# Transposing on VectorE in blocks of 32 instead of on TensorE, in a hybrid decoder step

## The chip, the cores and the metric

The kernel runs on one core of a Trainium2 chip. The metric is the device time of one execution in microseconds (us); lower is better. The core has five engines with a queue each: PE (TensorE, matmuls; its weight loads are shown as PEld), DVE (VectorE), ACT (ScalarE), POOL (GpSimd) and SP (SyncE, which here issues nearly all transfers). An engine works its queue in order and waits on semaphores where an operand or a buffer is not ready.

## The reference, cut to what matters

One step of a decoder layer with two head groups: 512 prompt tokens in one sequence, and 8 x 8 sample tokens with a past of 1024 positions each in a paged cache.

```
h = rms_norm(x, norm_in);  z = h @ w_in          # all branches from one projection (2048 -> IN_WIDTH)
attention heads (8 x 128): indexer scores -> top-k mask -> softmax -> @ v     # prompt, and samples with their cache
GLA heads (4 of 128 x 256): S = exp(last)*S + (k*exp(last-cum))^T v ;  o = (q*exp(cum)) S + (masked q k decay) v
y = rms_norm(x + concat(att * silu(ga), rms_norm(o, gla_norm) * silu(gb)) @ w_out, norm_f)
```

It returns y for prompt and samples, the new keys and values and the new states. The change touches the samples' softmax weights on their way to the product with v, the GLA heads' outputs on their way to the gate, and the store of the samples' y.

## The kernel before, in words

**Projection.** Activations stand transposed (features on partitions; 576 columns: 512 prompt, 64 sample). `gemm(b)` makes one block of 128 output features with matmuls of 128x288, each product in three terms (high and low halves of both operands, line L222); a weight tile of 128x512 serves 24 of them. The v columns are made the other way round with matmuls of 512 columns (L616 to L618). `wload` brings each weight tile: SP loads `w_raw` (L178), ACT rounds it to `w_hi` (L181), DVE makes the rest `w_lo` (L184); there are 3 raw buffers and 5 of each half.

**Sample units.** `units(un, hg, pages)` runs for `hg` 0 and 1 and in each for `w` 0 and 1: four units, each with 128 rows (4 heads x 32 sample rows) by 1088 columns (1024 of the past, 64 own). The scores `pS` are copied to `pr`, one ACTIVATE takes the exponentials with their sum (L813), nine PE transposes of 128x128 turn them (L821 eight times, L824 once) into PSUM tiles `pt`, three ACT copies (L822, L825) bring them to `prT`, and the `pOs` matmuls (L255, L258) multiply them with v.

**GLA heads.** `recur(h)` runs for h = 0 to 3. Its first half is the chain over the prompt's four chunks (`pUg` L1113, `pO`, state `Sst`). Then for each of the eight sample sequences b:

```
Kb = gl.tile([96, P], F32R, name="Kb", bufs=2)
ve.tensor_scalar(out=Kb, in0=ks[b // 4]..., scalar1=bm[...], op0=ALU.mult)        # L1145, DVE
pe.matmul(pU[:, :DV], Kb, vs[b // 4], start=True, stop=True)                       # L1146, PE: pUg
ve.scalar_tensor_tensor(out=st[:, m, :], in0=st[:, m, :], ..., in1=pU[:, :DV])     # L1147, DVE: st
```

With two buffers the `Kb` of a sequence can be made when the `pUg` two before it is done. The head ends with five scalings of `osb` (L1156, DVE), ten PE transposes (L1161 eight times, L1164 twice), four ACT activations into `oT` (L1162, L1165; tag e0, two buffers) and two stores `so` into scratch memory (SP). `gate(i)` later loads them again as `mo` into buffers of the same tag e0 (SP, L948) and multiplies them into `og` (POOL, L949). The decays `lv_d` that the next head's `pl` matmuls read are made on POOL (L969, L970), ACT (L971) and DVE (L1028, L1029).

**End.** The output projection writes the rows `y` in five row tiles, the sample rows last; each is normalised and stored in pieces of 512 columns (L1312 on DVE, L1314 on ACT, stores L1315).

**Order.** A tile scheduler fixes each engine's order when the kernel is built, from a timeline of its own and from priorities (`wload` goes ahead); nothing is reordered on the chip. PE, DVE, ACT, POOL and SP each follow their list.

Of the kernel before, what the change touches and what calls it, by code (L numbers as in the profile page):

```python
# [10 lines left out]
F32 = mybir.dt.float32  # L11
# [4 lines left out]
AF = mybir.ActivationFunctionType  # L16
ALU = mybir.AluOpType
AX = mybir.AxisListType
PSUM = bass.MemoryType.PSUM

P = 128
D = 2048
NK = D // P
TP = 512
# [95 lines left out]
def build(tc, I, O):  # L120
# [130 lines left out]
    def mm1(name):  # L251
        return pm.tile([P, 512], F32, name=name, tag="pm")
# [493 lines left out]

    mixS = gaS

    def units(un, hg, pages):


# [23 lines left out]
        for w in range(2):  # L775
            qz = ev.tile([P, 4, 4, 32], F32, name="qz", tag="e0", bufs=2)
            po_.memset(qz, 0.0)
            for g in range(4):
                src = qaS[:, 4 * hg + g, 32 * w : 32 * w + 32].rearrange("p (b t) -> p b t", t=DT)
                dst = qz[:, g].rearrange("p b t -> p (b t)")  # L780
                dst = bass.AP(tensor=dst.tensor, offset=dst.offset, ap=[dst.ap[0], [40, 4], [1, DT]])
                po_.tensor_copy(dst, src)
            pr = un.tile([P, PAST + TS], F32, name="pr")
            mx = un.tile([P, 8], F32, name="mxs", bufs=2)
            lsel = [selw[:, 256 * half + P * w : 256 * half + P * (w + 1)] for half in range(2)]
            for half in range(2):
                S = pm.tile([P, 512], F32, name="pS", tag="pu", bufs=1)
                pe.matmul(S, lsel[half], biasS[:, :512], start=True, stop=False)
                mms = []
                for bb in range(4):  # L790
                    k4 = kv[bb].rearrange("p j (g s) -> p j g s", g=4)
                    mms[:0] = [
                        partial(pe.matmul, S[32 * g : 32 * g + 32], qz[:, g, bb, :], k4[:, :, g, :], start=False, stop=(bb == 0), tile_position=(0, 32 * g))
                        for g in range(4)
                    ]
                run(*mms)
                yield
                kv = fetch(w, half, 1 - half)
                se.copy(pr[:, 512 * half : 512 * half + 512], S)
                ve.reduce_max(out=mx[:, half : half + 1], in_=pr[:, 512 * half : 512 * half + 512], axis=AX.X)  # L800
                if not half:
                    yield from rest(3)
            S = pm.tile([P, 512], F32, name="pS", tag="pu", bufs=1)
            pe.matmul(S[:, :TS], lsel[1], biasS[:, 512:], start=True, stop=False)
            run(*(
                partial(pe.matmul, S[32 * g : 32 * g + 32, :TS], qaS[:, 4 * hg + g, 32 * w : 32 * w + 32], kaS[:, 4 * hg + g, :], start=False, stop=True, tile_position=(0, 32 * g))
                for g in range(4)
            ))
            se.copy(pr[:, PAST:], S[:, :TS])
            ve.reduce_max(out=mx[:, 2:3], in_=pr[:, PAST:], axis=AX.X)  # L810
            ve.reduce_max(out=mx[:, 3:4], in_=mx[:, 0:3], axis=AX.X)
            ve.tensor_scalar(out=mx[:, 3:4], in0=mx[:, 3:4], scalar1=-SCALE, scalar2=None, op0=ALU.mult)
            se.activation(pr, pr, AF.Exp, bias=mx[:, 3:4], scale=SCALE, accum_out=mx[:, 4:5])  # L813
            ve.reciprocal(out=mx[:, 7:8], in_=mx[:, 4:5])
            yield
            prT = un.tile([P, 9, P], F32, name="prT")
            for c in range(3):
                pt = mm1("pt")
                if c < 2:
                    for j in range(4):  # L820
                        pe.transpose(pt[:, P * j : P * (j + 1)], pr[:, 512 * c + P * j : 512 * c + P * (j + 1)], ident)  # L821
                    se.copy(prT[:, 4 * c : 4 * c + 4, :], pt.rearrange("p (j r) -> p j r", j=4))  # L822
                else:
                    pe.transpose(pt[:, :P], pr[:, PAST + TS - P :], ident)  # L824
                    se.copy(prT[:, 8, :], pt[:, :P])  # L825
            yield from rest(2)
            pO = pm.tile([P, 512], F32, name="pOs", tag="pu", bufs=1)
            for half in range(2):
                mms = []
                for j in range(4):  # L830
                    mms[:0] = [
                        partial(
                            pe.matmul, pO[32 * g : 32 * g + 32].rearrange("p (b d) -> p b d", b=4), prT[:, 4 * half + j, 32 * g : 32 * g + 32],
                            kv[j][:, :, P * g : P * (g + 1)], start=(not half and j == 3), stop=False, tile_position=(0, 32 * g),
                        )
                        for g in range(4)
                    ]
                if half:
                    mms += [
                        partial(  # L840
                            pe.matmul, pO[32 * g : 32 * g + 32].rearrange("p (b d) -> p b d", b=4), prT[:, 8, 32 * g : 32 * g + 32],
                            vaS[:, P * h : P * (h + 1)].unsqueeze(1).to_broadcast([P, 4, P]), start=False, stop=True, tile_position=(0, 32 * g),
                        )
                        for g in range(4) for h in (4 * hg + g,)
                    ]
                run(*mms)
                yield
                if not half:
                    kv = fetch(w, 1, 1)
                    yield from rest(3)  # L850
                elif w == 0:
                    kv = fetch(1, 0, 0)
            ob = pr[:, :512]
            se.activation(ob, pO, AF.Copy, scale=mx[:, 7:8])
            pt = mm1("pt")
            for bb in range(4):
                pe.transpose(pt[:, P * bb : P * (bb + 1)], ob[:, P * bb : P * (bb + 1)], ident)
            src = bass.AP(tensor=pt.tensor, offset=pt.offset, ap=[pt.ap[0], [32, 4], [P + DT, 4], [1, DT]])
            sl = (slice(None), slice(4 * hg, 4 * hg + 4), slice(32 * w, 32 * w + 32))
            ve.tensor_tensor(  # L860
                out=mixS[sl].rearrange("p g (b t) -> p g b t", t=DT), in0=src,
                in1=gaS[sl].rearrange("p g (b t) -> p g b t", t=DT), op=ALU.mult,
            )
            yield from rest(2 + (w < hg))
# [227 lines left out]
    def recur(h, eL, qE, kDt, ks):  # L1092
# [61 lines left out]
        ve.reciprocal(out=ss, in_=ss)  # L1154
        for i in range(5):
            ve.tensor_scalar(out=osb[:, i, :], in0=osb[:, i, :], scalar1=ss[:, i : i + 1], scalar2=None, op0=ALU.mult)  # L1156
        for half in range(2):
            o_t = ev.tile([P, T], F32, name="oT", tag="e0", bufs=2)
            pt = mm1("pt")
            for i in range(4):  # L1160
                pe.transpose(pt[:, P * i : P * (i + 1)], osb[:, i, P * half : P * (half + 1)], ident)  # L1161
            se.activation(o_t[:, :TP], pt, AF.Copy, scale=gnorm[:, half : half + 1])  # L1162
            pt = mm1("pt")
            pe.transpose(pt[:, :P], osb[:, 4, P * half : P * (half + 1)], ident)  # L1164
            se.activation(  # L1165
                o_t[:, TP:T].rearrange("p (m c) -> p m c", m=4), pt[:, :P].rearrange("p (m c) -> p m c", m=4)[:, :, 0:16],
                AF.Copy, scale=gnorm[:, half : half + 1],
            )
            sy.dma_start(spill_o[2 * h + half], o_t)
# [73 lines left out]
    mg_s.close()  # L1243
    fp, fp_s = pool("fin", 1, side="right")
    y = [[None] * 5 for _ in range(4)]
    for n in range(20):
        if n < 16:
            y[n // 5][n % 5] = xp.tile([P, T], F32, name="y", tag=("xh", "xl")[n % 2])
        else:
            y[n // 5][n % 5] = fp.tile([P, 512], F32, name=f"y{n}")  # L1250
# [31 lines left out]
    for q, (c0, n) in enumerate(CH):  # L1282
# [14 lines left out]
        for i in range(5):  # L1297
# [5 lines left out]
            if last:  # L1303
# [2 lines left out]
                se.activation(yr[:r, i : i + 1], yr[:r, i : i + 1], AF.Sqrt, bias=eps[:r], scale=1.0 / D)  # L1306
                ve.reciprocal(out=yr[:r, i : i + 1], in_=yr[:r, i : i + 1])
                dst = O["yp"][P * i : P * (i + 1), :] if i < 4 else O["ys"]
                for c in range(4):
                    yc = y[c][i][:r, :512]  # L1310
                    if c < 2:
                        ve.tensor_scalar(out=yc, in0=yc, scalar1=yr[:r, i : i + 1], scalar2=None, op0=ALU.mult)  # L1312
                    else:
                        se.activation(yc, yc, AF.Copy, scale=yr[:r, i : i + 1])  # L1314
                    (sy, sy, se, sy)[c].dma_start(dst[:, 512 * c : 512 * c + 512], yc)  # L1315
# [79 lines left out]
```

## Time and profile before

| | |
|---|---|
| median of 3 runs | 1227.73 us (1227.54 to 1228.92) |
| profiled execution | 1227.91 us, span of its trace 1226.1 us, mean TensorE clock 0.998 |
| PE busy | 1212.5 us (99%) |
| DVE, ACT, POOL busy | 662.0 us (54%), 561.9 us (46%), 300.3 us (24%) |

The span runs from the first to the last instruction of the core. Busy time counts an engine's instructions, not its waits. Times in the trace are counted from the span's start. In a timeline a row is the start, the length, engine, line, operation and operands; `x8` puts consecutive equal instructions together, and the brackets behind it give the idle time before and what ended it.

### The profile page before, as it was taken

The page shows a single profiled execution, that of the slowest core. Times are in us where ns is not written, and L with a number is a line of the kernel's source. Part 1 is how long each engine was busy: PE and PEld are TensorE (multiplying, and loading weights), DVE is VectorE, ACT ScalarE, POOL GpSimd, SP SyncE. Part 2 cuts the span into 40 slices and gives each one's busy share as a digit, 9 for nine tenths or more (in the row PEclk, how much of TensorE's full clock was granted, in tenths as well). Part 3 has the DMA queues.
Part 4 walks back from the last instruction along what each step waited for, and adds up shares of the span by engine and source line. Part 5 has one row for each costly group of instructions (what it writes and reads, how often), then busy time and mean ns, then how long its engine had stood idle before and what let it go on. Part 6 is the DMA issues. An engine that isn't in the chain of part 4 may idle for free.

```text
span 1226.1 us, 23589 instructions
## 1 busy us (share of the span) xinstructions
PE 1212.5 (99%) x8693; PEld 1072.7 (87%) x8699; DVE 662.0 (54%) x1327; ACT 561.9 (46%) x1076; POOL 300.3 (24%) x471
## 2 busy tenths in 40 slices
PE   9999999999999999999999999999999999999997
PEld 8999987899997879998887788688899998888897
DVE  6777899699843314444436344436465552223233
ACT  6986655453443323443335363454466542223234
POOL 2225666446411201010104220302124010202021
PEclk9999999999999999999999999999999999999999
DMA  9643233423457586665557583677435544333335
GB/s 307 241 130 102 72 107 102 161 86 105 148 188 240 188 297 214 217 215 182 187 195 231 195 314 128 229 259 229 134 100 164 171 152 136 107 97 122 89 115 176
DMA packets 126885, 209.42 MB, mean 171 GB/s; under 512 B 14497, under 2 KB 37554, under 8 KB 126066
## 3 DMA queue, kind: packets, MB, share of 16 engines
q1 hardware_dynamic: 125826, 206.60, 50.9%
q8 instruction: 68, 1.11, 0.4%
q10 hardware_dynamic: 944, 1.32, 0.3%
q14 instruction: 47, 0.39, 0.1%
HBM read 184.52 MB, written 23.22 MB: 169 GB/s over the span
## 4 chain that ended last, share of the span: by engine, by line
PE 90%; DVE 5%; DMA 3%; ACT 1%; issue 1%; POOL 0%; SPq 0%; DVEq 0%; ACTq 0%; POOLq 0%
PE ps_g L222 37%; PE ps_g L230 6%; PE acc L1261 5%; PE acc L1259 5%; PE acc L1260 5%; PE ps_g L616 5%; PE ps_g L617 5%; PE ps_g L618 5%; PE pOs L258 2%; PE pS L258 2%; PE acc L1264 1%; PE acc L1263 1%; DMA xr<-in_xT 1%; PE ps_v L612 1%; PE ps_v L613 1%; DVE wk L505 1%
## 5 line engine op out<-in xcount | busy, mean ns | idle before, releaser
L181 ACT CAST w_hi<-w_raw 128x512 fp32r<-128x512 f32 x316 | 194.0, 619 | 360.5 <-PE ps_g L222 126.3
L184 DVE TENSOR_TENSOR w_lo<-w_raw,w_hi 128x512 fp32r<-128x512 f32 x252 | 180.1, 718 | 320.5 <-ACT w_hi L181 317.9
L222 PE MATMUL ps_g<-xl,w_hi 128*128 128x288 f32 x1312 | 289.0, 299 | 0.0
L222 PE MATMUL ps_g<-xh,w_hi 128*128 128x288 f32 x1312 | 288.2, 299 | 0.3 <-ACT xh L211 0.3
L222 PE MATMUL ps_g<-xh,w_lo 128*128 128x288 f32 x1312 | 286.0, 297 | 0.0
L222 PEld LDWEIGHTS ps_g<-xh,w_hi 128*128 128x128 f32 x1312 | 213.0, 189 | 6.0 <-issue 2.5
L222 PEld LDWEIGHTS ps_g<-xl,w_hi 128*128 128x128 f32 x1312 | 213.4, 189 | 1.7 <-issue 0.4
L222 PEld LDWEIGHTS ps_g<-xh,w_lo 128*128 128x128 f32 x1312 | 212.5, 188 | 0.6
L1260 PE MATMUL acc<-w_lo,mh 128*128 128x512 f32 (+1 forms) x320 | 110.7, 346 | 0.0
L1261 PE MATMUL acc<-w_hi,ml 128*128 128x512 f32 (+1 forms) x320 | 110.7, 346 | 0.0
L1259 PE MATMUL acc<-w_hi,mh 128*128 128x512 f32 (+1 forms) x320 | 110.3, 346 | 0.0
L616 PE MATMUL ps_g<-w_hi,xh 128*128 128x512 f32 x256 | 101.4, 397 | 0.0
L184 POOL TENSOR_TENSOR w_lo<-w_raw,w_hi 128x512 fp32r<-128x512 f32 x64 | 86.3, 1351 | 60.9 <-ACT w_hi L181 47.6
L617 PE MATMUL ps_g<-w_lo,xh 128*128 128x512 f32 x256 | 100.2, 391 | 0.0
L618 PE MATMUL ps_g<-w_hi,xl 128*128 128x512 f32 x256 | 99.8, 390 | 0.0
L1279 POOL TENSOR_TENSOR y<-y,nfb 128x512 f32<-128x512 f32 (+3 forms) x25 | 27.5, 1113 | 190.1 <-ACT yjk L1278 190.1
L1260 PEld LDWEIGHTS acc<-w_lo,mh 128*128 128x128 f32 x320 | 60.5, 189 | 7.5
L1259 PEld LDWEIGHTS acc<-w_hi,mh 128*128 128x128 f32 x320 | 60.4, 189 | 7.5
L1261 PEld LDWEIGHTS acc<-w_hi,ml 128*128 128x128 f32 x320 | 60.4, 189 | 7.5
L616 PEld LDWEIGHTS ps_g<-w_hi,xh 128*128 128x128 f32 x256 | 48.1, 188 | 12.7 <-issue 1.7
L618 PEld LDWEIGHTS ps_g<-w_hi,xl 128*128 128x128 f32 x256 | 48.1, 188 | 10.1
L617 PEld LDWEIGHTS ps_g<-w_lo,xh 128*128 128x128 f32 x256 | 48.1, 188 | 9.4
(340 smaller groups left out, 1941.7 us busy)
## 6 DMA issues: line engine op xcount, KB each, us to landing
w_raw<-in_w SPq DMA_DIRECT2D x188, 256.0 KB, 2.9
kt<-in_ck SPq DMA_DIRECT2D x128, 256.0 KB, 5.3
vt<-in_cv SPq DMA_DIRECT2D x128, 256.0 KB, 5.3
w_raw<-in_wv SPq DMA_DIRECT2D x64, 256.0 KB, 3.0
w_raw<-in_wo SPq DMA_DIRECT2D x64, 256.0 KB, 2.7
xr<-in_xT SPq DMA_DIRECT2D x16, 288.0 KB, 4.8
xt<-in_xp SPq DMA_DIRECT2D x4, 1024.0 KB, 5.5
sv<-v_tok SPq DMA_DIRECT2D x16, 256.0 KB, 4.9
```

What stands on the lines that cost most here:

```text
L181: c = se.copy(hi, raw)
L184: lo_eng[0].tensor_tensor(out=lo, in0=raw, in1=hi.bitcast(F32), op=ALU.subtract)
L222: pe.matmul(ps[:, j, :HT], wt, xt[:, j * HT : (j + 1) * HT], start=(k == 0 and n == 0), stop=(k == NK - 1 and n == 2),)
L230: pe.matmul(ps[:, 0, :TQ], wt[:, c], xt[:, P:T], start=(k == 0 and n == 0), stop=(k == NK - 1 and n == 2))
L258: f()
L616: pe.matmul(accs[i], xh[k][:, c], wh, start=a, stop=False)
L617: pe.matmul(accs[i], xh[k][:, c], wl, start=False, stop=False)
L618: pe.matmul(accs[i], xl[k][:, c], wh, start=False, stop=b)
L1259: pe.matmul(acc, mh[k][:, tsl], wh, start=(k == 0), stop=False)
L1260: pe.matmul(acc, mh[k][:, tsl], wl, start=False, stop=False)
L1261: pe.matmul(acc, ml[k][:, tsl], wh, start=False, stop=(k == NK - 1))
L1279: po_.tensor_tensor(out=yc, in0=yc, in1=nfb[:r, cs], op=ALU.mult)
```

## The change

- `blocks32` is new: 16 DVE transposes, each of a strip of 32 partitions whose blocks of 32 columns it turns.
- Units: `pr` gets 64 zero columns (POOL) between the past and the own columns, so that it is nine tiles of 128; the exponentials are two ACTIVATEs whose sums one DVE addition joins; `blocks32` of 32x9x32 writes `prT` in place of nine PE transposes and three ACT copies.
- Heads: `blocks32` of 32x8x32 writes the four prompt chunks of `osb` into the buffer of `vtok`, another of 32x2x32 writes the sample rows into that of `kDt`; the `oT` activations read those, so the next head's load into `vtok` and copy into `kDt` wait for them. Ten PE transposes per head go.
- End: the samples' `y` is one tile; 1152 columns are scaled on DVE and stored by SP, 896 on ACT and stored by ACT's queue.

```diff
+    def blocks32(out, src):
+        for a in range(4):
+            for c in range(4):
+                ve.transpose(out[32 * c : 32 * c + 32, :, 32 * a : 32 * a + 32], src[32 * a : 32 * a + 32, :, 32 * c : 32 * c + 32])
...
-            pr = un.tile([P, PAST + TS], F32, name="pr")
+            pr = un.tile([P, PAST + P], F32, name="pr")
+            po_.memset(pr[:, PAST : PAST + TS], 0.0)
...
-            se.activation(pr, pr, AF.Exp, bias=mx[:, 3:4], scale=SCALE, accum_out=mx[:, 4:5])
+            se.activation(pr[:, :PAST], pr[:, :PAST], AF.Exp, bias=mx[:, 3:4], scale=SCALE, accum_out=mx[:, 4:5])
+            se.activation(own_p, own_p, AF.Exp, bias=mx[:, 3:4], scale=SCALE, accum_out=mx[:, 5:6])
+            ve.tensor_tensor(out=mx[:, 4:5], in0=mx[:, 4:5], in1=mx[:, 5:6], op=ALU.add)
...
-            for c in range(3):
-                pt = mm1("pt")
-                if c < 2:
-                    for j in range(4):
-                        pe.transpose(pt[:, P * j : P * (j + 1)], pr[:, 512 * c + P * j : 512 * c + P * (j + 1)], ident)
-                    se.copy(prT[:, 4 * c : 4 * c + 4, :], pt.rearrange("p (j r) -> p j r", j=4))
-                else:
-                    pe.transpose(pt[:, :P], pr[:, PAST + TS - P :], ident)
-                    se.copy(prT[:, 8, :], pt[:, :P])
+            blocks32(prT, pr.rearrange("p (j s) -> p j s", s=P))
...
+        flat = lambda x: x.rearrange("p i d -> p (i d)").rearrange("p (j t) -> p j t", t=P)
+        blocks32(flat(vtok), flat(osb[:, :4]))
+        blocks32(kDt[:, :2], flat(osb[:, 4:]))
+        turn = flat(vtok).rearrange("p (i two) t -> p two i t", two=2)
         for half in range(2):
             o_t = ev.tile([P, T], F32, name="oT", tag="e0", bufs=2)
-            pt = mm1("pt")
-            for i in range(4):
-                pe.transpose(pt[:, P * i : P * (i + 1)], osb[:, i, P * half : P * (half + 1)], ident)
-            se.activation(o_t[:, :TP], pt, AF.Copy, scale=gnorm[:, half : half + 1])
-            pt = mm1("pt")
-            pe.transpose(pt[:, :P], osb[:, 4, P * half : P * (half + 1)], ident)
+            se.activation(o_t[:, :TP].rearrange("p (i t) -> p i t", t=P), turn[:, half], AF.Copy, scale=gnorm[:, half : half + 1])
...
+                if i == 4:
+                    for c, eng in ((slice(0, 1152), sy), (slice(1152, D), se)):
+                        yc = y_smp[:r, c]
...
+                        eng.dma_start(dst[:, c], yc)
+                    break
```

The lines of the changed kernel are numbered anew: `pUg` is L1148 there, `Kb` L1147, `st` L1149, the transposes L753.

The first place is DVE in head 0, from the five scalings of `osb` on. Before:

```order
L1156 TENSOR_SCALAR osb<-osb,ss 128x256 x5
L1147 SCALAR_TENSOR_TENSOR st<-st,eL,pUg 128x256
L1145 TENSOR_SCALAR Kb<-ks_8251,c_bm 96x128
L1147 SCALAR_TENSOR_TENSOR st<-st,eL,pUg 128x256
L1145 TENSOR_SCALAR Kb<-ks_8251,c_bm 96x128
L184 TENSOR_TENSOR w_lo<-w_raw,w_hi 128x512
L960 TENSOR_TENSOR kT<-ps_g,rstd 128x576
L1147 SCALAR_TENSOR_TENSOR st<-st,eL,pUg 128x256
L1145 TENSOR_SCALAR Kb<-ks_8252,c_bm 96x128
```

In the changed kernel, the same place:

```order
L1158 TENSOR_SCALAR osb<-osb,ss 128x256 x5
L753 STREAM_TRANSPOSE vtok<-osb 32x8x32
L1149 SCALAR_TENSOR_TENSOR st<-st,eL,pUg 128x256
L1147 TENSOR_SCALAR Kb<-ks_8260,c_bm 96x128
L753 STREAM_TRANSPOSE vtok<-osb 32x8x32 x7
L1149 SCALAR_TENSOR_TENSOR st<-st,eL,pUg 128x256
L1147 TENSOR_SCALAR Kb<-ks_8260,c_bm 96x128
L184 TENSOR_TENSOR w_lo<-w_raw,w_hi 128x512
L753 STREAM_TRANSPOSE vtok<-osb 32x8x32 x8
L753 STREAM_TRANSPOSE kDt<-osb 32x2x32 x3
L184 TENSOR_TENSOR w_lo<-w_raw,w_hi 128x512
L1149 SCALAR_TENSOR_TENSOR st<-st,eL,pUg 128x256
```

The transposes stand between the pairs of `st` and `Kb`; behind the last row follow a `Kb`, ten transposes of 32x2x32, `st`, `Kb`, three transposes, and only then `kT`.

The second place is POOL between heads 2 and 3, where it makes head 3's decays and multiplies the first gate. Before:

```order
L969 TENSOR_TENSOR lv_d<-cum 128x72x4
L970 TENSOR_TENSOR lv_d<-cum 128x72x4
L949 TENSOR_TENSOR og_11439<-og_11439,mo 128x576
L969 TENSOR_TENSOR lv_d<-cum 128x144x2
L970 TENSOR_TENSOR lv_d<-cum 128x144x2
L969 TENSOR_TENSOR lv_d<-cum 128x288
L970 TENSOR_TENSOR lv_d<-cum 128x288
```

In the changed kernel:

```order
L972 TENSOR_TENSOR lv_d<-cum 128x32x8
L951 TENSOR_TENSOR og_11509<-og_11509,mo 128x576
L971 TENSOR_TENSOR lv_d<-cum 128x72x4
L972 TENSOR_TENSOR lv_d<-cum 128x72x4
L971 TENSOR_TENSOR lv_d<-cum 128x144x2
L972 TENSOR_TENSOR lv_d<-cum 128x144x2
L971 TENSOR_TENSOR lv_d<-cum 128x288
```

The gate's product moved ahead of the pair of 128x72x4, so six decays instead of four follow it (the last, L972 of 128x288, is the next row).

The third place is SP at the same time (`so4` and `so5` are the two stores of head 2's `oT`). Before:

```order
L1097 DMA vtok_11885<-sv3_476 128x4x256
L178 DMA w_raw_12058<-in_w 128x512
L1134 DMA st_11940<-in_state 128x4x256
L178 DMA w_raw_12088<-in_w 128x512
L1148 DMA out_ss<-st_11216 512x1x256
L178 DMA w_raw_12118<-in_w 128x512
L1169 DMA so4_481<-oT_11279 128x576
```

In the changed kernel:

```order
L178 DMA w_raw_12146<-in_w 128x512
L1136 DMA st_12010<-in_state 128x4x256
L178 DMA w_raw_12176<-in_w 128x512
L1099 DMA vtok_11955<-sv3_476 128x4x256
L178 DMA w_raw_12206<-in_w 128x512
L1170 DMA so4_481<-oT_11363 128x576
L1170 DMA so5_482<-oT_11367 128x576
```

The load of `vtok` moved behind two weight loads and a state load; a third weight load stands behind it.

## Rows read from the trace of the kernel before

**Rows 1.** Page, parts 1 and 4: busy time; shares of the chain by engine.
```profile
PE 1212.5 (99%) x8693; PEld 1072.7 (87%) x8699; DVE 662.0 (54%) x1327; ACT 561.9 (46%) x1076; POOL 300.3 (24%) x471
...
PE 90%; DVE 5%; DMA 3%; ACT 1%; issue 1%; POOL 0%; SPq 0%; DVEq 0%; ACTq 0%; POOLq 0%
```

**Rows 2.** One line's instructions: a unit's transposes, ns min/median/max.
```profile
L821 PE MATMUL pt<-c_ident,pr x32: 270/272/302, 418.9 to 816.5; 128*128 128x128 f32 x32
```

**Rows 3.** Timeline of PE in the first unit (start us, length us).
```profile
418.70 0.39 PE L616 MATMUL ps_g<-w_hi,xh 128*128 128x512 f32 x1
418.93 1.03 PE L821 MATMUL pt<-c_ident,pr 128*128 128x128 f32 x8
...
420.03 0.39 PE L618 MATMUL ps_g<-w_hi,xl 128*128 128x512 f32 x1
```

**Rows 4.** Timeline of PE in the third unit.
```profile
680.20 0.63 PE L821 MATMUL pt<-c_ident,pr 128*128 128x128 f32 x4 [0.97 <-ACT lv_d L971]
```

**Rows 5.** DVE durations (ns), two timelines, and a group's busy us and mean ns.
```profile
L1123 DVE COPY Sst<-pUg x4: 409/416/418, 732.5 to 940.4; 128x256 f32<-128x256 f32 x4
...
674.93 0.41 DVE L1028 TENSOR_TENSOR lv_d<-lv_d,kT 128x256 f32<-128x256 f32 x1
675.27 0.41 DVE L1029 TENSOR_TENSOR lv_d<-lv_d,qT 128x256 f32<-128x256 f32 x1
...
771.51 0.59 DVE L1013 TENSOR_TENSOR ks<-kDs,ks 32x128 fp32r<-32x128 f32 x2
...
L1013 DVE TENSOR_TENSOR ks<-kDs,ks x8: 280/284/674, 672.5 to 928.0; 32x128 fp32r<-32x128 f32 x8
...
L1029 DVE TENSOR_TENSOR lv_d<-lv_d,qT 128x256 f32<-128x256 f32 x16 | 8.7, 556 | 1.6 <-ACT lv_d L971 1.6
```

**Rows 6.** Timelines of ACT and PE in the second unit.
```profile
540.56 0.18 ACT L813 ACTIVATION_READ_ACCUMULATOR pr<-pr,mxs 128x1 f32 x1
...
553.51 0.62 PE L255 MATMUL pOs<-vt,prT 128*32 128x512 f32 x1
```

**Rows 7.** Timelines of DVE and PE at the end of head 0.
```profile
744.89 1.40 DVE L1156 TENSOR_SCALAR osb<-osb,ss 128x256 f32<-128x256 f32 x5
746.20 0.48 DVE L1147 SCALAR_TENSOR_TENSOR st<-st,eL,pUg 128x256 f32<-128x256 f32 x1
746.60 0.28 DVE L1145 TENSOR_SCALAR Kb<-ks,c_bm 96x128 fp32r<-96x128 f32 x1
...
750.25 0.68 DVE L184 TENSOR_TENSOR w_lo<-w_raw,w_hi 128x512 fp32r<-128x512 f32 x1
...
745.89 0.28 PE L1146 MATMUL pUg<-vs,Kb 96*128 96x256 f32 x1
...
746.14 0.42 PE L222 MATMUL ps_g<-xl,w_hi 128*128 128x288 f32 x2
```

**Rows 8.** Timelines of PE, ACT, SP and POOL between heads 2 and 3.
```profile
910.76 0.28 PE L1146 MATMUL pUg<-vs,Kb 96*128 96x256 f32 x1
...
921.95 0.31 ACT L1165 ACTIVATE oT<-pt,gnorm 128x64 f32<-128x64 f32 x1
...
922.29 0.36 SPq L1169 DMA_DIRECT2D so<-oT  x1
...
925.88 0.32 SPq L948 DMA_DIRECT2D mo<-so  x1
...
930.17 1.42 POOL L949 TENSOR_TENSOR og<-og,mo 128x576 f32<-128x576 f32 x1 [1.62 <-DMA w_raw<-in_w]
...
932.40 0.88 POOL L970 TENSOR_TENSOR lv_d<-cum 128x288 f32<-128x288 f32 x1
...
938.25 0.18 PE L255 MATMUL pl<-lv_d 128*32 128x16 f32 x1 [0.54 <-DVE lv_d L1029]
```

**Rows 9.** Timeline of the tail, DVE and SP.
```profile
1220.21 0.88 DVE L1312 TENSOR_SCALAR y<-y,yr 64x512 f32<-64x512 f32 x2
1220.72 1.81 SPq L1315 DMA_DIRECT2D out_ys<-y  x3
```

More of the change, by code (lines that the diff above doesn't have):

```diff
@@ L808, in units @@
             ))
-            se.copy(pr[:, PAST:], S[:, :TS])
-            ve.reduce_max(out=mx[:, 2:3], in_=pr[:, PAST:], axis=AX.X)
+            own_p = pr[:, PAST + TS :]
+            se.copy(own_p, S[:, :TS])
+            ve.reduce_max(out=mx[:, 2:3], in_=own_p, axis=AX.X)
             ve.reduce_max(out=mx[:, 3:4], in_=mx[:, 0:3], axis=AX.X)
             ve.tensor_scalar(out=mx[:, 3:4], in0=mx[:, 3:4], scalar1=-SCALE, scalar2=None, op0=ALU.mult)
-            se.activation(pr, pr, AF.Exp, bias=mx[:, 3:4], scale=SCALE, accum_out=mx[:, 4:5])
+            se.activation(pr[:, :PAST], pr[:, :PAST], AF.Exp, bias=mx[:, 3:4], scale=SCALE, accum_out=mx[:, 4:5])
+            se.activation(own_p, own_p, AF.Exp, bias=mx[:, 3:4], scale=SCALE, accum_out=mx[:, 5:6])
+            ve.tensor_tensor(out=mx[:, 4:5], in0=mx[:, 4:5], in1=mx[:, 5:6], op=ALU.add)
             ve.reciprocal(out=mx[:, 7:8], in_=mx[:, 4:5])
@@ L1156, in recur @@
             ve.tensor_scalar(out=osb[:, i, :], in0=osb[:, i, :], scalar1=ss[:, i : i + 1], scalar2=None, op0=ALU.mult)
+        flat = lambda x: x.rearrange("p i d -> p (i d)").rearrange("p (j t) -> p j t", t=P)
+        blocks32(flat(vtok), flat(osb[:, :4]))
+        blocks32(kDt[:, :2], flat(osb[:, 4:]))
+        turn = flat(vtok).rearrange("p (i two) t -> p two i t", two=2)
         for half in range(2):
             o_t = ev.tile([P, T], F32, name="oT", tag="e0", bufs=2)
-            pt = mm1("pt")
-            for i in range(4):
-                pe.transpose(pt[:, P * i : P * (i + 1)], osb[:, i, P * half : P * (half + 1)], ident)
-            se.activation(o_t[:, :TP], pt, AF.Copy, scale=gnorm[:, half : half + 1])
-            pt = mm1("pt")
-            pe.transpose(pt[:, :P], osb[:, 4, P * half : P * (half + 1)], ident)
+            se.activation(o_t[:, :TP].rearrange("p (i t) -> p i t", t=P), turn[:, half], AF.Copy, scale=gnorm[:, half : half + 1])
             se.activation(
-                o_t[:, TP:T].rearrange("p (m c) -> p m c", m=4), pt[:, :P].rearrange("p (m c) -> p m c", m=4)[:, :, 0:16],
+                o_t[:, TP:T].rearrange("p (m c) -> p m c", m=4), kDt[:, half].rearrange("p (m c) -> p m c", m=4)[:, :, 0:16],
                 AF.Copy, scale=gnorm[:, half : half + 1],
@@ L1245, in build @@
     y = [[None] * 5 for _ in range(4)]
+    y_smp = fp.tile([P, D], F32, name="ysmp")
     for n in range(20):
-        if n < 16:
+        if n % 5 == 4:
+            y[n // 5][4] = y_smp[:, 512 * (n // 5) : 512 * (n // 5) + 512]
+        elif n < 16:
             y[n // 5][n % 5] = xp.tile([P, T], F32, name="y", tag=("xh", "xl")[n % 2])
@@ L1308, in build @@
                 dst = O["yp"][P * i : P * (i + 1), :] if i < 4 else O["ys"]
+                if i == 4:
+                    for c, eng in ((slice(0, 1152), sy), (slice(1152, D), se)):
+                        yc = y_smp[:r, c]
+                        if c.start:
+                            se.activation(yc, yc, AF.Copy, scale=yr[:r, i : i + 1])
+                        else:
+                            ve.tensor_scalar(out=yc, in0=yc, scalar1=yr[:r, i : i + 1], scalar2=None, op0=ALU.mult)
+                        eng.dma_start(dst[:, c], yc)
+                    break
                 for c in range(4):
```

## The prediction, made blind

> **What bounds the kernel now.** I read the page first: TensorE (PE) is busy 1212.5 of 1226.1 us and holds 90% of the chain that ended last, while VectorE (DVE) is busy for 54% of the span [rows 1]. So there is one question for every edit: does it shorten PE's in-order row of matmuls, and does PE still find its operands ready? Then I read PE's timeline around the transposes that go, DVE's durations for work like the work that comes, and the places where PE waits for DVE in program order. The profiled execution took 1227.91 us, 0.18 us above the median of the runs (1227.73); sums are made against it.
>
> **What PE sheds.** The diff takes 4 x 9 transposes out of the sample units and 4 x 10 out of the heads: 76. One lasts 272 ns [rows 2], but PE pipelines them, so duration is the wrong price. In [rows 3] the eight of a unit start at 418.93 and the second matmul behind them at 420.03; a 512-column matmul costs 0.23 (418.70 to 418.93), so eight took 420.03 - 418.93 - 0.23 = 0.87 us, 0.109 each. 76 x 0.109 = 8.3 us. In the third unit PE stood idle for 0.97 us in front of the second four [rows 4]; this wait belongs to the transposes and goes with them, if nothing else stands in the same place: -1.0. The twelve copies that ACT loses are not on the chain (ACT holds 1% of it).
>
> **What DVE gets: price.** 64 transposes of 32 partitions x 288 elements in the units, 64 of 256 and 64 of 64 in the heads. The trace of before has no transpose on DVE. Single-pass instructions of that length are the nearest: a COPY of 128x256 takes 0.416 and a subtraction of 32x128 takes 0.28 [rows 5]; the step between them, 0.14 per 128 elements, puts one of 64 elements at 0.21. The open point is whether consecutive ones overlap. Two of 128x256 with all partitions start 0.34 apart though each lasts 0.41; two on 32 partitions whose rows change took 0.59 together, that is 0.31 apart at 0.28 each: not overlapped, 0.03 between [rows 5]. In `blocks32` every instruction writes another 32 rows than the one before. So the bounds are 0.335 and 0.135 (256 and 64 elements, 0.08 under the durations) if they overlap, and 0.445 and 0.245 if they do not; I take 0.44 and 0.24, because the second pair of rows is the one with changing partitions. The Trainium skill, "VectorE: DVE Perf Modes", section "Two Vector instructions with no wait between them", has it as a model that an instruction whose input or output starts in another group of 32 partitions starts only when the earlier ones have finished. By that model the held price holds for all 192; by overlap the heads' part below would cost 0.9 instead of 6.2 us. The same page, "Rules for kernel authors", sends a 128x128 transpose to TensorE where PSUM will do, which speaks against the change.
>
> **Units.** 16 x (288/256 x 0.42 + 0.03), about 8 us of DVE (the 0.42 of a 256-element one scaled up), lies between the exponentials' end and the first matmul that reads `prT`. In the shortest of the four that is 540.74 to 553.51 [rows 6], 12.8 us. Small work between (one or two `w_lo`) leaves over 3 us. The `w_lo` behind are made up to 8 us later; with five buffers at 24 x 0.13 us = 3.1 us per tile there are some 12 us ahead. Cost 0 (gone cover: 1 us for each us). The second ACTIVATE, the add and the memset are 12 small instructions on engines that are half idle, also 0.
>
> **Heads: Kb behind transposes.** This is the first place where the change pays. PE's `pUg` waits for `Kb`, made on DVE, and in the new order the transposes stand ahead of the `Kb` (first pair of pieces of the order). Head 0 replayed: the scalings end at 744.89 + 1.40 = 746.29 and the fourth `pUg` starts at 745.89 [rows 7]. Per instruction I use start-to-start times: `st` 0.40 (746.20 to 746.60), and by the same overlap of 0.08 `Kb` 0.20 and `w_lo` 0.60. DVE: one transpose, st, Kb, seven, st, Kb: 746.29 + 8 x 0.44 + 2 x 0.60 = 751.0. Then w_lo, eight of 0.44, three of 0.24, w_lo, st, Kb: +1.2 + 3.5 + 0.7 + 0.6 = 757.0. Then ten of 0.24, st, Kb: 760.0. PE, by its new order at 0.13 (288 columns: two of 0.29 last 0.42 together [rows 7]), 0.23 and 0.12 (`pUg`) per matmul, reaches the four `pUg` that need them at 3.6, 7.5, 10.1 and 10.2 us after the fourth: 749.5, 753.4, 756.0, 756.1. The third waits 1.1 and the last 2.9 more: 4.0 us of idle PE. The same replay of heads 1, 2 and 3, whose fourth `pUg` are followed by 14.5, 14.7 and 13.9 us of matmuls up to the eighth instead of 10.2, gives 0.6, 0.7 and 0.9. Sum +6.2. With the overlapping price it is 0.9 (head 0 alone), at 0.40/0.20 it is 2.8.
>
> **Head 3: the gate's load.** The second place. In before, ACT's first `oT` of head 2 ends at 921.95 + 0.31 = 922.26, its store `so` issues at 922.29, the load `mo` waits for that store's landing (same buffers, tag e0) and issues at 925.88, POOL multiplies `og` at 930.17, then come four `lv_d` instructions, and through ACT and DVE the block `pl` of PE starts at 938.25, already 0.54 late [rows 8]. So `oT` to `pl` takes 16.0 us. Now `oT` needs all 32 transposes: my replay has head 2's last one at 927.1, `oT` at 927.4. POOL's `og` moves ahead of two more `lv_d` instructions (second pair of pieces), 1.7 us at the 0.88 that such a one takes in [rows 8]. `pl` can start at 927.4 + 16.0 + 1.7 = 945.1. PE reaches it later too: from the head's fourth `pUg`, at 910.76 [rows 8], it worked 27.0 us in before (938.25 - 910.76 - 0.54), and counted at the same prices the new order holds 1.9 us more, so with 0.7 of waits 910.76 + 28.9 + 0.7 = 940.4. Idle 4.7, of which 0.5 was there: +4.2. With overlapping transposes the last ends at 923.7 and the excess is 1.5.
>
> SP too: `vtok`'s load waits for `oT` and one `w_raw` is queued behind it (third pair); it moves from 921.1 to about 925, which five tiles of 3.1 us cover. Cost 0, up to 2 us if that cover is gone.
>
> **Tail.** Now 64x512 pieces, two on DVE in 0.88 us and two on ACT beside them, while SP issues three stores in a row until 1220.72 + 1.81 = 1222.5 [rows 9]. The change scales 1152 columns on DVE (about 1.0) and 896 on ACT (about 1.1) and issues one store on each queue: issued by about 1221.9. Gain 0.6 at most; fewer, larger stores land later. I take -0.3, bounds -0.6 and +0.5.
>
> **Sum.** 1227.9 - 8.3 - 1.0 - 0.3 + 6.2 + 4.2 = 1228.7; less the 0.2 to the median, 1228.5. The prices 0.44 and 0.24 are at the upper end of their bounds, so I round down and give 1228.
>
> **Rivals.**
> - *Overlapping transposes.* 1227.9 - 9.6 + 0.9 + 1.5 = 1220.7, 0.6% faster. For it: DVE overlaps most of its work [rows 5]. Against: the one pair on changing partitions. At 0.40/0.20 the same working gives 1224.5; below 0.41 the gain is large enough to be told from none.
> - *Dearer transposes.* DVE's work stretches when POOL moves data: `lv_d` of 128x256 runs at 0.41 alone but averages 0.56 over its 16 [rows 5]. From 0.46/0.26 on the heads pay 8.6 and the load 4.2, which gives 1231 and decides for slower. At 0.50/0.30 it is 1236; at 0.67/0.35 (the elements at half the rate, which no row shows) the heads alone cost 27 us and the end is at 1250.
> - *Nothing changes on PE's path at all*, because other waits take up what the transposes leave: this is what the forecast amounts to, and not apart from it.
>
> **How the numbers follow.** Forecast (not overlapped, 0.40 to 0.455): chance 0.58, own range 1224 to 1231, with 0.12 of it faster, 0.28 the same, 0.18 slower. Overlapping: 0.27, nearly all faster (0.26). Dearer: 0.15, nearly all slower (0.14). A difference of 0.2% (2.5 us) is about what a measurement here tells from none. Faster 0.38, same 0.30, slower 0.32. The range 1219.5 to 1235 leaves out the dear end of the third case (some 0.08) and the edges of the others.
>
> **What would show it.** `L1148 pUg` waiting for DVE `Kb`, 3 to 5 us in head 0 and about 1 us in each other head; `pl` of head 3 waiting for `lv_d`, 4 to 5 us; no `pOs` wait in a unit; the transposes' rows at 0.42 us with starts 0.44 apart. PE's busy time should fall by about 8 us whatever the end does. I am wrong if the starts are 0.34 apart (then 1220), if the `pUg` waits are absent, or if `mo` lands earlier than 7.9 us after `oT`.

## The result and the profile after

The changed kernel takes 1237.9 us (median of 6 runs, 1234.61 to 1240.64) against 1227.94 (6 runs, 1227.39 to 1228.92): ratio 1.0077, 95% interval 1.0061 to 1.0094. It is slower, and outside the stated range of 1219.5 to 1235. The profiled execution took 1235.84 us, 7.93 more than that of before.

The page's busy times and the engines' shares of the chain, to be read beside [rows 1]:

```profile
PE 1208.1 (98%) x8623; PEld 1067.4 (86%) x8623; DVE 735.3 (60%) x1522; ACT 558.2 (45%) x1071; POOL 302.0 (24%) x475
...
PE 84%; DVE 9%; issue 2%; DMA 2%; ACT 2%; SPq 1%; POOL 1%; POOLq 0%; DVEq 0%; ACTq 0%
```

PE is busy 4.4 us less, where the 76 transposes were worth 8.3, and DVE's share of the chain went from 5% to 9%. The view of waits lists what PE waited for (us in total, times, longest):

```profile
PE pUg L1148 <- DVE Kb L1147: 5.9, 7, 2.3
PE pl L255 <- DVE lv_d L1031: 4.1, 1, 4.1
PE pOs L255 <- DMA vt<-in_cv: 2.8, 1, 2.8
PE ps_g L617 <- DVE w_lo L184: 1.6, 1, 1.6
PE ps_idle L264 <- DVE sst L360: 1.1, 1, 1.1
PE pv L713 <- DVE tl L709: 0.8, 1, 0.8
PE ps_g L230 <- ACT raw L272: 0.5, 1, 0.5
PE pt L1005 <- DVE st L1149: 0.4, 1, 0.4
PE ps_g L616 <- DVE kT L962: 0.2, 1, 0.2
PE ps_g L222 <- ACT xh L211: 0.2, 1, 0.2
```

These are 17.6 us. The same view of before sums to 5.3 us, with the waits of [rows 4] and [rows 8] in it. So waits grew by 12.3, busy time fell by 4.4, and 12.3 - 4.4 = 7.9 is the whole difference. The first two lines were forecast (6.2 and 4.7). The third, where the prediction named "no `pOs` wait in a unit" as a sign, the fourth, and the missing 3.9 us of PE's saving were not.

Most of the missing saving is the clock's. Windows of 2 us (window, length, PE busy, granted clock, DMA share, GB/s) behind the idle stretches of head 0 and head 3:

```profile
756.00:758.00 2.00, 0.03 (x1) 0.56 0.24 90
758.00:760.00 2.00, 1.49 (x6) 0.50 0.00 0
760.00:762.00 2.00, 2.00 (x5) 0.50 0.86 317
762.00:764.00 2.00, 2.00 (x8) 0.74 0.73 244
946.00:948.00 2.00, 1.27 (x119) 0.84 0.38 130
948.00:950.00 2.00, 2.00 (x40) 0.50 0.39 131
950.00:952.00 2.00, 2.00 (x14) 0.80 0.04 9
```

0.50 is 1.2 GHz of 2.4. Busy time times the missing share of the clock is 0.7 + 1.0 + 0.5 us in the first place and 0.2 + 1.0 + 0.4 in the second, 3.8 us together, about what PE's busy time lacks. That the two agree so closely is in part luck, because PE's row also became shorter in a place that I did not forecast. Before, the scheduler had put the heads' `kD` transposes into the middle of the fourth unit's 32 score matmuls, which take 766.73 to 773.09:

```profile
766.73 1.05 PE L255 MATMUL pS<-kt,qz 128*32 128x512 f32 x2
767.71 0.66 PE L999 MATMUL pt<-c_ident,kD 128*128 128x128 f32 x4
...
773.09 0.50 PE L612 MATMUL ps_v<-w_hi,xs 128*128 128x512 f32 x1
```

In the changed kernel the scheduler's new order leaves the 32 in one piece, 768.85 to 772.42:

```profile
768.85 0.62 PE L255 MATMUL pS<-kt,qz 128*32 128x512 f32 x1
...
772.42 0.66 PE L1001 MATMUL pt<-c_ident,kD 128*128 128x128 f32 x4
```

That is 6.36 us against 3.57; less the five transposes of before at 0.109, some 2.2 us are saved. About as much must have been added to PE's busy time elsewhere, and where is not shown.

Ahead of the first fall PE had stood idle for 1.63 us, and a stretch of 2.25 us had just begun:

```profile
752.46 0.39 PE L616 MATMUL ps_g<-w_hi,xh 128*128 128x512 f32 x1
754.48 0.50 PE L617 MATMUL ps_g<-w_lo,xh 128*128 128x512 f32 x1 [1.63 <-DVE w_lo L184]
...
755.74 0.29 PE L1148 MATMUL pUg<-vs,Kb 96*128 96x256 f32 x1
758.28 0.58 PE L1148 MATMUL pUg<-vs,Kb 96*128 96x256 f32 x1 [2.25 <-DVE Kb L1147]
```

DVE in the same microseconds, to be read beside [rows 7]:

```profile
744.88 3.13 DVE L753 STREAM_TRANSPOSE vtok<-osb 32x256 f32<-32x256 f32 x7
...
749.35 3.59 DVE L753 STREAM_TRANSPOSE vtok<-osb 32x256 f32<-32x256 f32 x8
752.97 0.73 DVE L753 STREAM_TRANSPOSE kDt<-osb 32x64 f32<-32x64 f32 x3
753.73 0.69 DVE L184 TENSOR_TENSOR w_lo<-w_raw,w_hi 128x512 fp32r<-128x512 f32 x1
...
755.04 2.48 DVE L753 STREAM_TRANSPOSE kDt<-osb 32x64 f32<-32x64 f32 x10
...
757.95 0.28 DVE L1147 TENSOR_SCALAR Kb<-ks,c_bm 96x128 fp32r<-96x128 f32 x1
```

Seven of 0.43 us take 3.13, so they start 0.45 apart; ten of 0.24 take 2.48, 0.25 apart. No transpose overlaps the one before. The `w_lo` at 753.73 stands behind eleven of them, and PE waits for it from 752.85; the `Kb` at 757.95, which ends the wait of 2.25 us, stands behind the ten.

In head 3 the chain came as forecast. SP, POOL and PE, beside [rows 8]:

```profile
929.24 0.80 SPq L1170 DMA_DIRECT2D so<-oT  x2
...
933.43 1.12 SPq L950 DMA_DIRECT2D mo<-so  x1
...
937.60 1.44 POOL L951 TENSOR_TENSOR og<-og,mo 128x576 f32<-128x576 f32 x1 [4.26 <-DMA mo<-so]
...
946.73 0.18 PE L255 MATMUL pl<-lv_d 128*32 128x16 f32 x1 [4.08 <-DVE lv_d L1031]
```

The gate's load ends the wait of POOL at 937.60, and PE stands still for 4.08 us.

### The profile page after: what moved, and what is told of

Read it like the earlier page. It is cut to its first block, busy times and chain, and to the rows that moved or that the text cites. A ratio compares the mean times of both kernels' runs of the same rounds, so it can differ in the third digit from the quotient of the medians.

```text
span 1234.1 us, 23640 instructions
## 1 busy us (share of the span) xinstructions
PE 1208.1 (98%) x8623; PEld 1067.4 (86%) x8623; DVE 735.3 (60%) x1522; ACT 558.2 (45%) x1071; POOL 302.0 (24%) x475
## 4 chain that ended last, share of the span: by engine, by line
PE 84%; DVE 9%; issue 2%; DMA 2%; ACT 2%; SPq 1%; POOL 1%; POOLq 0%; DVEq 0%; ACTq 0%
PE ps_g L222 33%; PE ps_g L230 6%; PE acc L1265 5%; PE acc L1263 5%; PE acc L1264 5%; PE ps_g L616 4%; PE ps_g L617 4%; PE ps_g L618 4%; PE pOs L258 2%; DVE vtok L753 2%; PE pS L258 1%; DVE kDt L753 1%; PE acc L1268 1%; PE acc L1267 1%; PE ps_v L613 1%
## 5 line engine op out<-in xcount | busy, mean ns | idle before, releaser
L1283 POOL TENSOR_TENSOR y<-y,nfb 128x512 f32<-128x512 f32 (+1 forms) x20 | 22.3, 1125 | 173.9 <-ACT yjk L1282 173.9
```

## The experiments

Twelve kernels ran. Times are medians, ratios are to the kernel before on the same chip. The changed kernel did not run beside them, so differences from it compare two sets of runs; the kernel before took 1227.9 to 1228.4 in all of them. Each edit also makes the scheduler place some other instructions anew, so a difference in time can hold more than the edit.

**Parts alone.** Three kernels have one part of the change each; the edit is that part of the diff. The units:

> Only the units' part of the change. My theory (the loss sits in the heads): PE loses 36 transposes (3.9 us) and the 0.97 us wait in the third unit, DVE's transposes hide, but the third unit's second pOs block meets its vt loads again (2.8 us in the changed kernel): about 1226, 1224 to 1227. Rival (more work on DVE delays weights everywhere, so the units lose too): 1230 or more.

Measured: 1228.97 us (12 runs, 1225.29 to 1231.03), ratio 0.9999 (0.9989 to 1.0010). Neither: the gain that I expected is absent, but so is a loss. The trace says where it went. PE's timeline in the second and the third unit:

```profile
551.49 0.62 PE L255 MATMUL pOs<-vt,prT 128*32 128x512 f32 x1
...
710.85 0.59 PE L255 MATMUL pOs<-vt,prT 128*32 128x512 f32 x1 [3.37 <-DMA vt<-in_cv]
```

In the second unit PE is at 551.49 where [rows 6] has 553.51: 2.0 us gained by two units, 0.109 for each transpose as priced. In the third it comes to its first `pOs` block 4.2 us earlier than before, and then waits 3.37 us for the second block's values from the cache: that block starts at 710.85 against 711.61, so only 0.8 us of the 4.2 is left. The first blocks, before and in the units alone:

```profile
693.61 0.62 PE L255 MATMUL pOs<-vt,prT 128*32 128x512 f32 x1
...
689.41 0.62 PE L255 MATMUL pOs<-vt,prT 128*32 128x512 f32 x1
```

The loads of `vt` came only 1.4 us earlier, and the last one no earlier. SP's row of loads and its longest wait between 670 and 706 us, first before, then in the units alone:

```profile
695.75 9.54 SPq L157 DMA_DIRECT2D vt<-in_cv  x15
SPq L178 <- DVE w_lo L184: 13.3, 5, 5.7
...
694.35 11.07 SPq L157 DMA_DIRECT2D vt<-in_cv  x15
SPq L178 <- DVE w_lo L184: 15.2, 5, 10.9
```

Before, SP also waited 2.1 us at these loads for PE to free their buffers. In the units alone that wait is gone: the weight loads (L178) ahead of them on SP wait up to 10.9 us for a `w_lo`, which now stands behind the unit's transposes on DVE. The profile of the whole change shows the same 10.9. So the order on SP keeps the loads from following PE; how much of the 3.37 us it causes, and how much the transfers themselves, was not tested.

The heads:

> Only the heads' part. My theory: -4.4 us of transposes, +5.9 pUg waits, +3.6 at pl of head 3, +2 at weights behind transposes, and 4 us because PE's granted clock falls to half after the longest idle stretches: 1227.9 + 11 = 1239, 1236 to 1241. Rival (the units cost): within 2 us of before.

Measured: 1237.67 us (5 runs, 1237.22 to 1238.39), ratio 1.0070 (1.0056 to 1.0083). As my theory has it: the loss sits in the heads.

The result rows:

> Only the samples' result rows in one tile with two stores. From the two traces the time from the last matmul's start to the span's end went from 8.36 to 8.61 us: 0 to +0.4 us, that is 1228.0 to 1228.3. Rival (my blind forecast): -0.3, down to -0.6.

Measured: 1228.74 us (11 runs), ratio 1.0001 (0.9992 to 1.0010). No difference that can be measured; the two expectations lie too close together to be told apart by it.

**The third unit's loads.** One block of PE is queued later, in the units alone and in the whole change (`latest` is the last projection matmul written before it):

```diff
-                run(*mms)
+                if half and hg and not w:
+                    with tc.issue_after(latest[0].ins):
+                        run(*mms)
+                else:
+                    run(*mms)
```

> Units' part alone, with the second pOs block of the third unit queued some 50 matmul rows later on PE. In the run of the units alone PE gained 1.0 us per unit up to 4.2 us, and 3.4 of them went into waiting for that block's vt loads. If those loads take the units' gain, the wait is gone now and the time is 1228.0 - 4.9 + 0.9 (pl of head 3 later) = 1224, 1223 to 1226. Rival (the gain is not there, since something else that is spread out limits the kernel): 1227.5 or more, with another wait in the place of this one.

Measured: 1221.37 us (6 runs, 1220.45 to 1222.67), ratio 0.9940 (0.9925 to 0.9955). It lies below what I expected. The wait for `vt` is gone from the view of waits. The gain over the units alone is 7.6 us, more than the 3.4 us of the wait. Some 2.2 us of it is the fourth unit's score row, which here is in one piece and in the units alone is not. The clock has a share too: the twelve runs of the units alone spread over 5.7 us, from a mean clock of 0.999 in the fastest to 0.995 in the slowest (0.004 of 1226 us is 4.9 us, an estimate), and these six, at 0.996 to 0.999, over 2.2. Where the clock fell in the slower runs isn't shown; the profiled one kept 1.00 behind the wait.

> The whole change, with the second pOs block of the third unit queued later, as in the run of that edit on the units alone. If the vt loads take 2.8 us and the half clock that follows the idle stretch in some executions 1 to 2 more, it gives 1237.9 - 4 = 1234, 1232 to 1235.5. Rival (the heads wait that much longer instead, since PE comes to them earlier): 1237 or more.

Measured: 1232.41 us (5 runs, 1231.90 to 1234.84), ratio 1.0037 (1.0023 to 1.0050): 5.5 us under the changed kernel. The loads are part of the loss; the rest stays, in the heads.

**The gate's load.** `mo` gets buffers of its own, nothing else:

```diff
-        o_t = ev.tile([P, T], F32, name="mo", tag="e0", bufs=2)
+        o_t = mg.tile([P, T], F32, name="mo", bufs=2)
```

> The whole change, but the gate's loads mo have two buffers of their own, so that the first no longer waits for head 2's oT to be stored. My theory: the 4.1 us wait of pl in head 3 and the half clock behind it (about 1.7 us) go: 1237.9 - 5.5 = 1232.4, 1230.5 to 1234. Rival (pl waits for lv_d behind DVE's transposes and not for the load): within 1 us of the changed kernel, 1237 to 1239.

Measured: 1232.34 us (12 runs, 1229.64 to 1234.73), ratio 1.0028 (1.0016 to 1.0040), 5.6 us under the changed kernel, as expected; the wait of `pl` fell from 4.1 to 0.8 us. So it waited for the load, by way of the buffers. Not all the rest came as I had it: the fall of the clock in head 3 is gone, but one stands behind the wait for `vt` in its place (0.91 from 700 to 720 us), and the `pUg` waits fell too, from 5.9 to 4.7 us, in another order of POOL and PE.

**Kb ahead of the transposes.** With `mo` as above, the transposes are queued behind the head's last `Kb`:

```diff
+        with tc.issue_after(getattr(last_kb, "ins", last_kb)):
             blocks32(flat(vtok), flat(osb[:, :4]))
             blocks32(kDt[:, :2], flat(osb[:, 4:]))
```

> The whole change, with two edits: mo has its own buffers, and the heads' transposes are queued on DVE behind the head's last Kb. If the pUg waits come from the transposes that stand ahead of Kb, and the half clock from the idle stretches, both vanish, the mean clock returns to 0.998, and what is left is -8.3 - 1.0 + 2.9 (vt loads) + 0.8 + 0.3: 1222 to 1224. Rival (DVE has too much work in the heads, whatever its order): the waits move to weights (w_lo) or to st, and the time stays at 1229 or more.

Measured: 1224.1 us (9 runs, 1223.03 to 1226.03), ratio 0.9966 (0.9954 to 0.9978), just above what I expected; the profile's mean clock is 0.996, not the 0.998 that I had. No `pUg` wait is left; `pl` of head 3 waits 3.3 us, for `lv_d` whose ACT step stands behind `oT`:

```profile
PE pl L255 <- DVE lv_d L1031: 3.3, 1, 3.3
PE pOs L255 <- DMA vt<-in_cv: 3.1, 1, 3.1
```

The heads' part alone with the same two edits:

> The heads' part alone, with mo in buffers of its own and the transposes behind the last Kb. -4.4 us of transposes, +3 at pl of head 3, nothing at pUg, the clock whole or nearly so: 1228.0 - 4.4 + 3 = 1226.6, 1225 to 1228, against 1237.7 for the heads' part as it stands. Rival (DVE is too full in the heads in any order): 1232 or more.

Measured: 1227.47 us (11 runs, 1226.33 to 1229.01), ratio 0.9992 (0.9983 to 1.0001): as my theory has it, and no gain that can be told from none.

All three edits with the whole change:

> The whole change with all three edits: mo in buffers of its own, the heads' transposes behind the last Kb, the second pOs block of the third unit later. 1224.1 - 3.1 (vt) - 1 to 2 (clock) = 1219 to 1220, with pl of head 3 still 3 us late. If the heads' transposes cost more than the 4.4 us that they free on PE, it stays at or above 1221.4, the time of the units with the later block.

Measured: 1225.99 us (8 runs, 1223.74 to 1227.99), ratio 0.9981 (0.9970 to 0.9991). A miss: removing the wait for `vt` made it no faster. PE now comes to head 0 earlier and waits there for another instruction behind transposes, `st`, which frees a PSUM bank. The clock falls there (0.83 from 750 to 760 us). The view of waits, and DVE:

```profile
PE pl L257 <- DVE lv_d L1037: 3.3, 1, 3.3
PE ps_v L614 <- DVE st L1155: 2.5, 1, 2.5
```

```profile
753.75 1.47 DVE L755 STREAM_TRANSPOSE kDt<-osb 32x64 f32<-32x64 f32 x6
755.25 0.48 DVE L1155 SCALAR_TENSOR_TENSOR st<-st,eL,pUg 128x256 f32<-128x256 f32 x1
```

So the rival that I had named for the run with two edits was half right: some of the wait moves to `st`. With the heads' transposes on DVE the kernel is 6.0 us slower than the version at the end of this section, which has the other two edits and leaves them on PE (the tail's part, in this kernel alone, is 0.2 of it).

**The clock.** In the whole change, 20 transposes of the identity, read by nobody, stand ahead of head 0's last `pUg`:

```diff
+                if h == 0 and b == 7:
+                    lead = pe.transpose(pU[:, DV : DV + P], ident, ident)
...
+                        for _ in range(19):
+                            lead = pe.transpose(pU[:, DV : DV + P], ident, ident)
```

> The whole change, with 20 more PE transposes of the identity, whose results nobody reads, queued ahead of head 0's last pUg, where PE stood idle for 2.4 us. If PE's granted clock falls because it stood idle, the clock stays whole here, the stretch of half clock behind it (758 to 763 us) goes, and more work makes the kernel faster: 1237.9 - 2.2 = 1235.7. Rival (the clock falls for another reason, as DVE's load): the same 1237.9 or up to 0.5 more.

Measured: 1233.82 us (9 runs, 1231.18 to 1238.79), ratio 1.0048 (1.0032 to 1.0064), 4.1 us under the changed kernel in the median, though the two ratios' intervals just touch. Head 0 in its windows:

```profile
756.00:758.00 2.00, 0.56 (x2) 1.00 0.73 240
758.00:760.00 2.00, 2.00 (x16) 1.00 0.52 153
760.00:762.00 2.00, 1.82 (x16) 1.00 0.00 0
762.00:764.00 2.00, 1.10 (x5) 1.00 0.40 154
```

The clock stays at 1.00 in head 0 with DVE as loaded as in the changed kernel (736.4 us busy against 735.3), so DVE's load isn't what lowers it, and filling PE's idle time kept it up. The nine runs have a mean clock of 0.994 to 0.999. How much of the 4.1 us is head 0's alone is open: the profiled execution, at 1235.65, is only 0.2 under the changed kernel's; four other transposes also moved ahead of that `pUg`; the second fall, in head 3, is absent in this profile, and another stands behind the wait for `vt` (0.50 from 712 to 714 us).

**Partitions.** The heads' transposes are issued in pairs that keep their partitions:

```diff
+        for a in range(4):
+            for c in range(4):
+                for out, src in ((flat(vtok), flat(osb[:, :4])), (kDt[:, :2], flat(osb[:, 4:]))):
+                    ve.transpose(out[32 * c : 32 * c + 32, :, 32 * a : 32 * a + 32], src[32 * a : 32 * a + 32, :, 32 * c : 32 * c + 32])
```

> The whole change, with the heads' transposes issued as pairs: one of 256 and one of 64 elements with the same input and output partitions behind each other. If a transpose waits for the earlier ones because its partitions change, the second of a pair starts 0.35 us after the first (0.08 before its end) in place of 0.45, the pUg waits shrink by 1 to 3 us, 1234 to 1237. Rival (DVE never overlaps transposes): all starts stay 0.45 and 0.25 us apart, and the time is 1237 to 1239.

Measured: 1235.67 us (4 runs, 1234.71 to 1236.21), ratio 1.0057 (1.0038 to 1.0076), within what I expected, but not told apart from the changed kernel by the time. DVE:

```profile
750.24 0.43 DVE L1163 STREAM_TRANSPOSE vtok<-osb 32x256 f32<-32x256 f32 x1
750.61 0.19 DVE L1163 STREAM_TRANSPOSE kDt<-osb 32x64 f32<-32x64 f32 x1
750.81 0.43 DVE L1163 STREAM_TRANSPOSE vtok<-osb 32x256 f32<-32x256 f32 x1
```

The second of a pair starts 0.37 us after the first, 0.06 before its end; the next pair, with other partitions, starts only when it has ended. A pair takes 0.57 us in place of 0.45 + 0.25. So it is the change of partitions that holds a transpose back, as the Trainium skill, "VectorE: DVE Perf Modes", section "Two Vector instructions with no wait between them", has it.

**A version that beats both.** The units' part with the later block, and `mo` in its own buffers; the heads transpose on PE as before:

> The units' part with the later block, and mo in buffers of its own; the heads as before. pl of head 3 waited 1.7 us there through so, mo and POOL; without that chain 1221.4 - 1.7 = 1219.7, 1219 to 1221. Rival (pl waits for DVE or ACT): 1221 to 1222.

Measured: 1219.95 us (5 runs, 1219.32 to 1220.51), ratio 0.9931 (0.9917 to 0.9944). 0.7% faster than the kernel before and 1.5% faster than the changed one. Some 2.2 of its 8.4 us under the kernel before are the score row in one piece, which the scheduler gave and no edit asked for.

## Why the prediction was wrong, step by step

- *What PE sheds.* Right. 0.109 us per transpose: two units gained 2.0 us, and with the wait of [rows 4] PE was 4.2 us ahead in the third. What I left out is that a new order can move other rows of PE: the score row became 2.2 us shorter.
- *Price of a transpose.* Right. 0.436 and 0.236 us long, 0.45 and 0.25 apart, against 0.44 and 0.24; no overlap, for the reason given, which the pairs bear out.
- *Units: cost 0.* **This step failed.** I set the later `w_lo` against PE's five buffers only, and `prT` and `w_lo` did come in time for PE there. I didn't follow `w_lo` to SP, whose weight loads wait for it with the loads of `vt` behind them, nor ask what a PE that is 4 us earlier runs into. The loads come only 1.4 us earlier, so PE waits 3.37 us for them in the units alone and 2.8 us in the changed kernel, where I had no `pOs` wait. With the block later, the units alone give 1221.4.
- *Heads: Kb behind transposes.* Right in mechanism, and in the sum: 5.9 us of waits against 6.2. That the sum came so close is partly luck, for by heads it is 2.3, 1.2, 1.0 and 1.4 against 4.0, 0.6, 0.7 and 0.9. The replay counted `w_lo` only as work of DVE, not as something PE waits for: 1.6 us more in head 0, and 0.6 for `kT` and `st`.
- *Head 3: the gate's load.* Right: 4.1 us of wait, forecast 4.7, and it is the gate's load, since buffers of its own take it away.
- *Tail.* Wrong in sign, and too small to measure by the time. The profiles show it: from the last matmul's start to the end it takes 8.57 us in the changed kernel and with the tail's part alone, against 8.39 before, so +0.2 (8.36 and 8.61 in the expectation come from rounded spans); I had -0.3.
- *What no step had:* the clock. **My sum priced idle time at its length, and this failed too.** In head 0 and head 3 PE's clock was 1.2 GHz for 6.8 and 3.4 us, and 3.8 us were lost by it. It does not follow every stretch: the 2.8 us before `vt` left the clock whole in this profile, while with `mo` in its own buffers the profile shows 0.91 for the 20 us around the same wait. Why a stretch brings it down in one execution and not in another is open.

The prediction's sum, 1228.7, stands for the profiled execution, which took 1235.84: 7.1 more. Waits grew by 12.3, where the sum had -1.0 + 6.2 + 4.2 = 9.4: 2.9 more, made of 2.8 for `vt` and 2.2 for `w_lo`, `kT` and `st`, less 0.9 by which `pUg` and `pl` fell short, and less some 1.2 of small waits that were there before. Busy time fell by 3.9 less than 8.3, which the clock's 3.8 and the shorter score row are part of. The tail makes 0.5. That is 7.3, and 0.2 is not placed. The median lies 2.1 above the profiled execution; the four longer runs had mean clocks of 0.992 to 0.993, this one 0.994, and a thousandth of the clock is 1.2 us of such a run (an estimate).

The rivals: transposes that overlap are refuted by every profile that has the order of the change. Dearer ones too: starts of 0.45 and 0.25 us stay under the 0.46 and 0.26 from which I called them dearer, and the kernel was slower at the price that I had forecast. The third, other waits that take up what the transposes leave, is what happened in the units: 3.4 of 4.2 us.

## What to carry to other kernels

When an engine that is busy 99% of the time gets less to do, look for whatever it reaches next in its order, transfers above all: saved time that ends in front of them is not saved, and a transfer can be held by another load ahead of it in its queue, here one that waited for DVE. Where an in-order engine takes over work in many small pieces, everything queued behind the pieces becomes late, not only the operand you were thinking of; ask it for each kind of instruction on that queue. And an idle stretch of TensorE can cost more than its length, through the clock: here filling one of 2.3 us with useless work kept the clock up there, and the median came out 4 us lower. Last, an edit makes the scheduler order other instructions anew: compare rows that it shouldn't have touched before its whole gain is put down to it.

## What the runs showed of the hardware

- PE's granted clock fell from 1.00 to 0.50, 1.2 GHz of 2.4, behind 1.6 us of idle and the start of another 2.25 us, and behind 4.1 us; it was 0.50 for 6.8 and 3.4 us. With the second stretch filled it did not fall there. Behind the wait for `vt`, of 2.8 to 3.4 us, it fell in three profiles and stayed at 1.00 in three others.
- DVE transposes of 32 partitions take 0.47, 0.436 and 0.236 us for 288, 256 and 64 elements of 4 bytes. They follow each other at 0.01 to 0.02 us when partitions change, and overlap by 0.06 us when they stay the same.
